# The up projection's gated convolution, four tiles at a time instead of two

## The chip, the cores and the metric

One core of a Trainium2 chip runs the whole kernel in one launch. The metric is the device time of that launch in microseconds (us). The core has a TensorE (matrix products), a VectorE, a ScalarE, a GpSimd and a SyncE (here it only issues transfers); each takes its own queue of instructions in order and waits on semaphores for the others.

## The reference, cut to what matters

One layer of an encoder on 256 positions of width 2048, all in float32: a token mixer, then a convolutional gated MLP with 5504 hidden channels, then a last norm. The change is in the MLP:

```python
def conv_ffn(x, g_norm, w_up, conv_k, conv_b, w_down):
    h = rms_norm(x, g_norm)
    up = h @ w_up                                   # 2048 -> 2 x 5504
    pad = jnp.pad(up, ((0, 0), (1, 1), (0, 0)))
    up = (pad[:, :t] * conv_k[0] + pad[:, 1:t + 1] * conv_k[1]
          + pad[:, 2:t + 2] * conv_k[2] + conv_b)   # width 3, over positions, each channel by itself
    gate, val = jnp.split(up, 2, axis=-1)
    return x + (jax.nn.silu(gate) * val) @ w_down
```

## The kernel before, in words

Every float32 operand of a product is split in two parts, a high part (rounded, `F32R`) and a low part (the rest), and three of the four products are summed. The activations' parts lie next to each other in SBUF. The weights are split as they come in, in pieces of 256 rows by 512 columns: SyncE loads a piece into `wraw` (five buffers), ScalarE copies the high part into `whi` (L171), VectorE subtracts it and writes the low part `wlo` (L172). There are four buffers each of `whi` and `wlo`; a piece is split three pieces ahead of its use.

The up stage works in 22 groups. A group takes the gate channels and the value channels of two neighbouring blocks of 128 (`nb` = 2; the last group has `nb` = 1), so four tiles of 128 channels by 256 positions, each in a PSUM bank of its own: columns 0 to 255 hold the sum for the high part of the activations (and, added to it, that of the low weights), columns 256 to 511 the sum for their low part. The contraction over 2048 goes in eight pieces; per piece there are high products (L223, 512 columns) and, every second piece, the low products of two pieces (L227, 256 columns). Eight banks let the next group start while the last is read out.

When a group's products are issued, `ev_up` reads its banks out and queues the rest as tasks of later pieces. For two blocks b = 0, 1, each with its gate tile and its value tile:

- read out, at once: ScalarE copies the second half of a bank into `tb`, VectorE adds the first half into `ta` (L1064, L1066), four times.
- `conv(0)` one piece into the next group, `conv(1)` three pieces into it (five in the last group): VectorE multiplies a tile by the norm's factor of each position (`rs["rb"]`, L1072), ScalarE makes the middle tap with the bias into `tc` (L1074), VectorE adds the two outer taps (L1077, L1079), for the two tiles of the block.
- `gate(b)` one piece after it: ScalarE applies SiLU (L1084), VectorE multiplies by the value tile (L1085).
- one piece later `split_plain` (L542, L543): the high and low part of the result, as activations of the down projection.
- for 13 of the pairs of blocks (`DOWN_PAIRS`) the sums that the down projection's faster scheme of multiplying 2 x 2 blocks needs are made two pieces after the gate (`act_blocks`, L324 to L327), split a piece later into the tile `so` and written to memory on GpSimd's queue (L1099).

Between these lie jobs that split some of the down projection's weights ahead of time (`split_ahead`): in eight groups a load on GpSimd's queue, then four additions on VectorE (L1296) at the pieces 6 and 7 of that group and 0 and 1 of the next, and two splits (L1301, L1302) at its pieces 2 and 4, by way of the same tile `so`.

The order of every engine's queue is the order in which the code issues. At each piece `begin` first issues the loads, then the split of the piece three ahead, then the tasks of this piece, and then the piece's products follow:

Of the kernel before, what the change touches and what calls it, by code (L numbers as in the profile page):

```python
# [8 lines left out]
F32 = mybir.dt.float32  # L9
BF16 = mybir.dt.bfloat16  # L10
F32R = mybir.dt.float32r
AF = mybir.ActivationFunctionType
OP = mybir.AluOpType
# [3 lines left out]
T = 256  # L17
# [8 lines left out]
NF = DFF // 128  # L26
# [53 lines left out]
def trunk_kernel(ctx, tc, x, x_t, vecs, w_in, ln_g, ln_b, w_st, b_s, rpb, w_branch, w_out, w_up, w_down,  # L80
                 norm_final, out):
    nc = tc.nc
    ctx.enter_context(tc.manual_schedule())

    def pool(name, side="left", bufs=1, space=None):
        kw = {} if space is None else {"space": space}
        st = ExitStack()
        p = st.enter_context(tc.tile_pool(name=name, bufs=bufs, side=side, reuse_waits="tile", **kw))
        return p, st
# [11 lines left out]
    turns, turns_st = pool("turns")  # L101
    turns = {"p": turns}
# [87 lines left out]
    def at(i, f):  # L190
        tasks.setdefault(i, []).append(f)

    cur = [0]
# [128 lines left out]
    def act_blocks(w, a11, a21, a12, a22):  # L322
        s3, n1, p2, s4 = (w[:, n * 128:(n + 1) * 128] for n in range(4))
        nc.vector.tensor_sub(s3, a11, a21)  # L324
        nc.vector.tensor_sub(n1, a22, a21)
        nc.vector.tensor_add(p2, n1, a11)
        nc.vector.tensor_sub(s4, a12, p2)  # L327
# [149 lines left out]
    ck = const.tile([128, 4, 2 * NF], F32)  # L477
# [63 lines left out]
    def split_plain(p, dst):  # L541
        nc.scalar.activation(dst[:, 0, :], p, AF.Copy)  # L542
        nc.vector.tensor_sub(dst[:, 1, :], p, dst[:, 0, :].bitcast(F32))  # L543
# [26 lines left out]
    def first_room(name, dt):  # L570
        return ypool.tile([128, 2, 512], dt, name=f"y{first_rooms.index('t13' if name == 'f' else name)}")
# [409 lines left out]
    rs = {}  # L981
# [73 lines left out]
    ff = {}  # L1055

    def ev_up(f0, nb):
        def done(ps, i):
            n = nb
            a = []  # L1060
            own = {}
            for p in ps:
                t = turns["p"].tile([128, T], F32, name="tb", bufs=3)
                nc.scalar.activation(t, p[:, T:], AF.Copy)  # L1064
                u = turns["p"].tile([128, T], F32, name="ta", bufs=6)
                nc.vector.tensor_add(u, p[:, :T], t)  # L1066
                a.append(u)

            def conv(b):
                c = []  # L1070
                for u, ch in ((a[b], f0 + b), (a[n + b], NF + f0 + b)):
                    nc.vector.tensor_mul(u, u, rs["rb"])  # L1072
                    v = ff["p"].tile([128, T], F32, name="tc", bufs=4)
                    nc.scalar.activation(v, u, AF.Identity, scale=ck[:, 1, ch:ch + 1], bias=ck[:, 3, ch:ch + 1])  # L1074
                    c.append((u, v, ch))
                for u, v, ch in c:
                    nc.vector.scalar_tensor_tensor(v[:, 1:], u[:, :T - 1], ck[:, 0, ch:ch + 1], v[:, 1:],  # L1077
                                                   op0=OP.mult, op1=OP.add)
                    nc.vector.scalar_tensor_tensor(v[:, :T - 1], u[:, 1:], ck[:, 2, ch:ch + 1], v[:, :T - 1],  # L1079
                                                   op0=OP.mult, op1=OP.add)  # L1080
                at(cur[0] + 1, lambda: gate(b, c[0][1], c[1][1]))

            def gate(b, g, v):
                nc.scalar.activation(g, g, AF.Silu)  # L1084
                nc.vector.tensor_mul(g, g, v)  # L1085
                at(cur[0] + 1, lambda: split_plain(g, ff["a"][f0 + b]))
                own[b] = g
                if b and f0 // 2 in ff["kept"]:
                    at(cur[0] + 2, sums)
                    at(cur[0] + 3, sums_split)  # L1090

            def sums():
                own["w"] = ff["more"].tile([128, 512], F32, name="sw")
                act_blocks(own["w"], *(own[k][:, t * 128:(t + 1) * 128] for k in range(2) for t in range(2)))

            def sums_split():
                o = ff["more"].tile([128, 2, 512], F32R, name="so")
                split_plain(own["w"], o)
                nc.gpsimd.dma_start(ff["kept"][f0 // 2], o.bitcast(F32))  # L1099

            at(i + 1, lambda: conv(0))
            if n > 1:
                at(i + (5 if f0 + 3 == NF else 3), lambda: conv(1))
        return done


# [107 lines left out]
    def sums_room(name, dt):  # L1214
        return s_room["p"].tile([128, 2, 512], dt, name=name)
# [15 lines left out]
    for n, (q, i, j) in enumerate(X_SUMS):  # L1231
        sum_acts_at(i, j, first_sums[2 * q], lambda q=q: q,
                    lambda name, dt, i=i: first_room("s2" if name == "f" and i < 16 else name, dt), f"s{n}", True)
# [17 lines left out]
    def split_read(kept, g, tile_of, queue=nc.gpsimd):  # L1251
        def read(pair, box, n):
            u = box.setdefault("u", [])
            u.append([tile_of(pair, p + n) for p in "hl"])
            for t, src in zip(u[-1], kept[pair, g][n]):
                queue.dma_start(t.bitcast(F32), src)
            if len(u) == 2:
                split_sums(box, u)
        return read

    def kept_sums(pair, box):
        held = [s for p, s in gate_held.values() if p == pair]
        if held:
# [11 lines left out]
                 split=(GATE_SPLIT[br], split_read(g_kept, br, lambda pair, name: sums_room("k" + name, F32R), nc.sync)))  # L1275
# [55 lines left out]
    for n, (pair, g) in enumerate((pair, g) for g in range(2) for pair in OUT_SPLIT[g]):  # L1331
        t_kept[pair, g] = split_rows("out", pair, g)
        i = g_at[2 * n][1]
# [46 lines left out]
    for n, q in enumerate(OUT_PAIRS):  # L1380
        i = g_m2[0][1] + OUT_SUMS[n]
# [3 lines left out]
    for f in range(0, NF, 2):  # L1385
        nb = min(2, NF - f)
# [17 lines left out]
    def down_order(g):  # L1404
# [7 lines left out]
                 split=({p: (6, 6) for p in DOWN_SPLIT}, split_read(d_kept, g, down_split_tile))) for g in range(2)]  # L1412
    ff["kept"] = {p: dram.tile([128, 2, 512], F32, name=f"sums{p}") for p in DOWN_PAIRS}
    for p, turn in zip(DOWN_SPLIT, DOWN_JOBS):
        for g in range(2):
            d_kept[p, g] = split_rows("down", p, g)
            i = g_up[turn[g]][1]
# [181 lines left out]
```

## Time and profile before

| what | us |
|---|---|
| device time, median of 3 runs | 1292.7 (1292.57 to 1293.34) |
| profiled execution, first to last instruction (span) | 1291.3 |
| TensorE busy | 1281.6 (99%) |
| VectorE busy | 1143.6 (89%) |
| ScalarE busy | 815.7 (63%) |
| GpSimd busy | 174.5 (14%) |
| up stage after its first group, 609 to 1066 us: TensorE, VectorE, ScalarE busy | 457.0, 407.5, 281.2 |

The profile is one execution, taken by the hardware profiler; of that execution only the span is known, and 1.4 us lie between it and the median of the timed runs. Times in its rows are us from the first instruction. PE is TensorE's products, PEld its weight loads, DVE VectorE, ACT ScalarE, POOL GpSimd, SP SyncE. A row of the timeline gives start, duration, engine, line, instruction, output<-inputs, shapes and count; in brackets the idle time before it and who ended it. Neighbouring instructions of an engine overlap a little, so a row of two is shorter than twice a row of one. A row of the groups gives the count, then busy us and the mean ns of one, then the idle time before them by who ended it. A row of the waits gives who waited for whom, us in all, times, and the longest.

### The profile page before, as it was taken

How to read it: one execution, taken by the hardware profiler on the slowest of the kernel's cores; microseconds unless marked ns; L12 is line 12 of the kernel's file. 1: busy time of each engine (PE TensorE's matmuls, PEld its weight loads, DVE VectorE, ACT ScalarE, POOL GpSimd, SP SyncE). 2: the span in 40 equal slices, each digit the busy share in tenths (PEclk: the TensorE clock that was granted, in tenths of full speed). 3: DMA queues.
4: the chain of work that ended last, by engine and by line, in shares of the span. 5: the costliest groups of instructions: out<-in, count | busy, mean ns of one | idle time of the engine just before them, and what ended most of it. 6: DMA issues, size and time to landing. Idle time of an engine off the chain costs nothing.

```text
span 1291.3 us, 19690 instructions
## 1 busy us (share of the span) xinstructions
PE 1281.6 (99%) x6653; PEld 1092.7 (85%) x6653; DVE 1143.6 (89%) x1712; ACT 815.7 (63%) x1229; POOL 174.5 (14%) x309
## 2 busy tenths in 40 slices
PE   9999999999999999999999999999999999999997
PEld 7888888888888888888888888888888888888885
DVE  7898978888889988996888899998988989989987
ACT  7776577877855655566566656566665656555554
POOL 0003706334000001100001001100000001211210
PEclk9999999999999999999999999999999999999999
DMA  9779879998799977965588788888877859998993
GB/s 368 273 272 282 289 236 306 322 316 300 275 335 349 353 244 244 412 225 164 182 295 274 239 297 290 270 267 285 266 220 222 279 171 363 368 388 325 353 383 146
DMA packets 199893, 369.51 MB, mean 286 GB/s; under 512 B 15984, under 2 KB 124144, under 8 KB 199792
## 3 DMA queue, kind: packets, MB, share of 16 engines
q1 hardware_dynamic: 175472, 286.36, 64.6%
q0 software_dynamic: 23888, 81.23, 17.8%
q8 instruction: 52, 0.85, 0.3%
q10 hardware_dynamic: 432, 0.66, 0.1%
q14 instruction: 49, 0.40, 0.1%
HBM read 320.48 MB, written 45.61 MB: 284 GB/s over the span
## 4 chain that ended last, share of the span: by engine, by line
PE 98%; DVE 1%; issue 0%; DVEq 0%; ACT 0%; ACTq 0%
PE bank L223 31%; PE bank L227 16%; PE bank L320 12%; PE bank L318 12%; PE bank L319 12%; PE bank L251 5%; PE bank L253 5%; PE bank L252 5%; PE bank L835 1%; DVE wlo L172 0%; PE bank L885 0%; PE bank L499 0%; PE bank L699 0%; PE bank L875 0%; PE bank L973 0%
## 5 line engine op out<-in xcount | busy, mean ns | idle before, releaser
L172 DVE TENSOR_TENSOR wlo<-wraw,whi 128x1024 fp32r<-128x1024 f32 (+1 forms) x472 | 537.0, 1151 | 98.2 <-ACT whi L171 64.2
L171 ACT ACTIVATE whi<-wraw 128x1024 fp32r<-128x1024 f32 (+1 forms) x472 | 463.3, 995 | 187.9 <-PE bank L319 72.4
L223 PE MATMUL bank<-h,whi 128*128 128x512 f32 x1760 | 425.5, 392 | 0.0
L223 PEld LDWEIGHTS bank<-h,whi 128*128 128x128 f32 x1760 | 322.0, 188 | 61.8
L227 PEld LDWEIGHTS bank<-h,wlo 128*128 128x128 f32 x1760 | 225.9, 191 | 8.8
L227 PE MATMUL bank<-h,wlo 128*128 128x256 f32 x1760 | 228.6, 283 | 0.0
L1074 ACT ACTIVATE tc<-ta,ck 128x256 f32<-128x256 f32 x86 | 47.1, 595 | 110.0 <-DVE ta L1072 110.0
L320 PE MATMUL bank<-wlo,a 128*128 128x512 f32 x188 | 73.4, 390 | 0.2 <-DVE wlo L172 0.2
L318 PE MATMUL bank<-whi,h 128*128 128x512 f32 x186 | 73.2, 394 | 0.0
L318 PE MATMUL bank<-whi,a 128*128 128x512 f32 x188 | 73.2, 389 | 0.0
L319 PE MATMUL bank<-whi,a 128*128 128x512 f32 x188 | 73.1, 389 | 0.0
L319 PE MATMUL bank<-whi,h 128*128 128x512 f32 x186 | 72.8, 391 | 0.0
L320 PE MATMUL bank<-wlo,h 128*128 128x512 f32 x186 | 72.6, 390 | 0.0
L1077 DVE SCALAR_TENSOR_TENSOR tc<-ta,ck,tc 128x255 f32<-128x255 f32 x86 | 41.4, 481 | 14.4 <-ACT tc L1074 14.4
L800 POOL TENSOR_SCALAR_AFFINE_SELECT bias<-run 64x128 f32<-64x128 f32 x64 | 39.7, 654 | 85.4 <-DVE sc L843 84.7
L1306 POOL DMA_DIRECT2D down_h<-so x16 | 8.7, 545 | 311.1 <-ACT tc L1084 170.3
L251 PE MATMUL bank<-whi,y 128*128 128x512 f32 x128 | 50.6, 395 | 0.0
L251 PE MATMUL bank<-whi,h 128*128 128x512 f32 x128 | 50.4, 394 | 0.0
L253 PE MATMUL bank<-wlo,h 128*128 128x512 f32 x128 | 49.9, 390 | 0.0
L253 PE MATMUL bank<-wlo,y 128*128 128x512 f32 x128 | 49.9, 390 | 0.0
L252 PE MATMUL bank<-whi,y 128*128 128x512 f32 x128 | 49.8, 389 | 0.0
L252 PE MATMUL bank<-whi,h 128*128 128x512 f32 x128 | 49.8, 389 | 0.0
(332 smaller groups left out, 2075.7 us busy)
## 6 DMA issues: line engine op xcount, KB each, us to landing
wraw<-in_w_up_dram SPq DMA_DIRECT2D x336, 256.0 KB, 4.0
wraw<-in_w_in_dram SPq DMA_DIRECT2D x107, 512.0 KB, 6.3
wraw<-in_w_down_dram SPq DMA_DIRECT2D x78, 512.0 KB, 7.3
wraw<-in_w_in_dram SPq DMA_DIRECT2D x70, 256.0 KB, 6.0
wraw<-in_w_branch_dram SPq DMA_DIRECT2D x32, 512.0 KB, 5.7
wraw<-in_w_out_dram SPq DMA_DIRECT2D x28, 512.0 KB, 6.1
h<-sums POOLq DMA_DIRECT2D x18, 512.0 KB, 7.6
tw<-in_w_down_dram POOLq DMA_DIRECT2D x8, 1024.0 KB, 8.3
```

The lines of the kernel that those rows point to most:

```text
L171: nc.scalar.activation(h[:, k, :m], w[:, k, :m], AF.Copy)
L172: nc.vector.tensor_sub(l[:, k, :m], w[:, k, :m], h[:, k, :m].bitcast(F32))
L223: nc.tensor.matmul(p, h[:, k - k0, b * 128:(b + 1) * 128], acts(k), start=k == 0, stop=k == nk - 1)
L227: nc.tensor.matmul(p[:, :T], l[:, k - k0, b * 128:(b + 1) * 128], acts(k)[:, 0, :], start=False, stop=False)
L251: nc.tensor.matmul(p, xh, h[:, kk, :m], start=st, stop=False)
L252: nc.tensor.matmul(p, xl, h[:, kk, :m], start=False, stop=False)
L253: nc.tensor.matmul(p, xh, l[:, kk, :m], start=False, stop=sp)
L318: nc.tensor.matmul(p, xh, h, start=st, stop=False, **kw)
L319: nc.tensor.matmul(p, xl, h, start=False, stop=False, **kw)
L320: nc.tensor.matmul(p, xh, l, start=False, stop=sp, **kw)
L1074: nc.scalar.activation(v, u, AF.Identity, scale=ck[:, 1, ch:ch + 1], bias=ck[:, 3, ch:ch + 1])
L1077: nc.vector.scalar_tensor_tensor(v[:, 1:], u[:, :T - 1], ck[:, 0, ch:ch + 1], v[:, 1:], op0=OP.mult, op1=OP.add)
```

## The change

The four tiles of a group go through the tail together. The copies from the banks go straight into one tile `ta` of 128 x 4 x 256 (one buffer instead of six, and no `tb`), and the additions are in place. One piece into the next group the four tiles are multiplied by the norm's factors in one operation, with the row of factors repeated by a step of zero, and ScalarE makes the four middle taps into one tile `tc` (one buffer). At the second piece VectorE adds the first outer tap of all four tiles, then the second of all four, and ScalarE's SiLU on both gate tiles at once follows in the same task. At the third piece come one product of gates and values and one copy of the high parts, at the fourth one subtraction for the low parts; for the kept pairs the sums at the fifth and their splitting and writing at the sixth, each a piece earlier than before. The last full group is no exception any more.

```diff
     def ev_up(f0, nb):
         def done(ps, i):
...
-            for p in ps:
-                t = turns["p"].tile([128, T], F32, name="tb", bufs=3)
-                nc.scalar.activation(t, p[:, T:], AF.Copy)
-                u = turns["p"].tile([128, T], F32, name="ta", bufs=6)
-                nc.vector.tensor_add(u, p[:, :T], t)
-                a.append(u)
...
-            at(i + 1, lambda: conv(0))
-            if n > 1:
-                at(i + (5 if f0 + 3 == NF else 3), lambda: conv(1))
+            u = turns["p"].tile([128, 2 * nb, T], F32, name="ta", bufs=1)
+            for n, p in enumerate(ps):
+                nc.scalar.activation(u[:, n], p[:, T:], AF.Copy)
+                nc.vector.tensor_add(u[:, n], p[:, :T], u[:, n])
+            box = {}
+            channels = [f + b for f in (f0, NF + f0) for b in range(nb)]
+
+            def scale():
+                rb = rs["rb"]
+                nc.vector.tensor_mul(u, u, bass.AP(tensor=rb.tensor, offset=rb.offset,
+                                                   ap=[rb.ap[0], [0, 2 * nb], [1, T]]))
+                v = box["v"] = ff["p"].tile([128, 2 * nb, T], F32, name="tc", bufs=1)
+                for n, ch in enumerate(channels):
+                    nc.scalar.activation(v[:, n], u[:, n], AF.Identity, scale=ck[:, 1, ch:ch + 1],
+                                         bias=ck[:, 3, ch:ch + 1])
+
+            def conv():
+                v = box["v"]
+                for tap, to, of in ((0, slice(1, T), slice(0, T - 1)), (2, slice(0, T - 1), slice(1, T))):
+                    for n, ch in enumerate(channels):
+                        nc.vector.scalar_tensor_tensor(v[:, n, to], u[:, n, of], ck[:, tap, ch:ch + 1], v[:, n, to],
+                                                       op0=OP.mult, op1=OP.add)
+                nc.scalar.activation(v[:, :nb], v[:, :nb], AF.Silu)
+
+            def gate():
+                v = box["v"]
+                nc.vector.tensor_mul(v[:, :nb], v[:, :nb], v[:, nb:])
+                a = ff["ap"][f0 // 2]
+                nc.scalar.activation(a[:, :, 0, :], v[:, :nb], AF.Copy)
+
+            def split():
+                v, a = box["v"], ff["ap"][f0 // 2]
+                nc.vector.tensor_sub(a[:, :, 1, :], v[:, :nb], a[:, :, 0, :].bitcast(F32))
...
+            steps = [scale, conv, gate, split]
+            if f0 // 2 in ff["kept"]:
+                steps += [sums, sums_split]
+            for n, step in enumerate(steps):
+                at(i + 1 + n, step)
         return done
```

`sums` and `sums_split` do what they did, on the new tile.

More of the change, by code (lines that the diff above doesn't have):

```diff
@@ L1058, in done @@
         def done(ps, i):
-            n = nb
-            a = []
-            own = {}
-            for p in ps:
-                t = turns["p"].tile([128, T], F32, name="tb", bufs=3)
-                nc.scalar.activation(t, p[:, T:], AF.Copy)
-                u = turns["p"].tile([128, T], F32, name="ta", bufs=6)
-                nc.vector.tensor_add(u, p[:, :T], t)
-                a.append(u)
[L1069 to L1090, printed above, removed]
+            u = turns["p"].tile([128, 2 * nb, T], F32, name="ta", bufs=1)
+            for n, p in enumerate(ps):
+                nc.scalar.activation(u[:, n], p[:, T:], AF.Copy)
+                nc.vector.tensor_add(u[:, n], p[:, :T], u[:, n])
@@ L1092, in sums @@
+            def split():
+                v, a = box["v"], ff["ap"][f0 // 2]
+                nc.vector.tensor_sub(a[:, :, 1, :], v[:, :nb], a[:, :, 0, :].bitcast(F32))
             def sums():
-                own["w"] = ff["more"].tile([128, 512], F32, name="sw")
-                act_blocks(own["w"], *(own[k][:, t * 128:(t + 1) * 128] for k in range(2) for t in range(2)))
+                v = box["v"]
+                box["w"] = ff["more"].tile([128, 512], F32, name="sw")
+                act_blocks(box["w"], *(v[:, k, t * 128:(t + 1) * 128] for k in range(2) for t in range(2)))
@@ L1096, in sums_split @@
             def sums_split():
                 o = ff["more"].tile([128, 2, 512], F32R, name="so")
-                split_plain(own["w"], o)
+                split_plain(box["w"], o)
                 nc.gpsimd.dma_start(ff["kept"][f0 // 2], o.bitcast(F32))
-            at(i + 1, lambda: conv(0))
-            if n > 1:
-                at(i + (5 if f0 + 3 == NF else 3), lambda: conv(1))
+            steps = [scale, conv, gate, split]
+            if f0 // 2 in ff["kept"]:
+                steps += [sums, sums_split]
```

## The prediction, made before the change was run

> **What bounds the kernel now.** I read the page first, then who waited for whom, the stage by itself, one group in order of time, and last the margins.
>
> ```profile
> span 1291.3 us, 19690 instructions
> PE 98%; DVE 1%; issue 0%; DVEq 0%; ACT 0%; ACTq 0%
> PE bank L499 <- DVE one L489: 1.5, 1, 1.5
> PE bank L320 <- DVE wlo L172: 0.2, 1, 0.2
> 609.00:1066.00 457.00, 457.00 (x2630) 403.89 (x2629) 407.50 (x693) 281.19 (x446) 29.64 (x53) 1.00 0.78 254
> ```
>
> The first two lines are the page's span and its chain of work: TensorE carries 98% of it. The next two are all the waits of TensorE in the run, 1.7 us. The last is the up stage after its first group (busy us of PE, weight load, DVE, ACT, POOL): TensorE is busy in all 457.0 us, VectorE in 407.5, ScalarE in 281.2. So no saving on VectorE or ScalarE can shorten this stage. The change can only do nothing or make TensorE wait, and the question is how much delay the split weights bear. They come three pieces ahead, and both engines take their queues in order. Here is group 7 (counted from 0; its pieces P0 to P7).
>
> ```profile
> 743.78 1.22 DVE L172 TENSOR_TENSOR wlo<-wraw,whi 128x1024 fp32r<-128x1024 f32 x1
> 745.52 1.41 DVE L1066 TENSOR_TENSOR ta<-bank,tb 128x256 f32<-128x256 f32 x4
> 746.31 2.00 ACT L171 ACTIVATE whi<-wraw 128x1024 fp32r<-128x1024 f32 x2
> 746.84 2.08 PE L227 MATMUL bank<-h,wlo 128*128 128x256 f32 x16
> 747.39 2.36 DVE L172 TENSOR_TENSOR wlo<-wraw,whi 128x1024 fp32r<-128x1024 f32 x2 [0.47 <-ACT whi L171]
> 749.67 0.75 DVE L1072 TENSOR_TENSOR ta<-ta,rb 128x256 f32<-128x256 f32 x2
> 750.12 1.10 ACT L1074 ACTIVATE tc<-ta,ck 128x256 f32<-128x256 f32 x2 [1.82 <-DVE ta L1072]
> 750.75 0.48 DVE L1077 SCALAR_TENSOR_TENSOR tc<-ta,ck,tc 128x255 f32<-128x255 f32 x1 [0.33 <-ACT tc L1074]
> 751.12 1.04 ACT L171 ACTIVATE whi<-wraw 128x1024 fp32r<-128x1024 f32 x1
> 751.27 0.48 DVE L1079 SCALAR_TENSOR_TENSOR tc<-ta,ck,tc 128x255 f32<-128x255 f32 x1
> 751.68 0.48 DVE L1077 SCALAR_TENSOR_TENSOR tc<-ta,ck,tc 128x255 f32<-128x255 f32 x1
> 752.07 0.40 ACT L1084 ACTIVATE tc<-tc 128x256 f32<-128x256 f32 x1
> 752.19 0.48 DVE L1079 SCALAR_TENSOR_TENSOR tc<-ta,ck,tc 128x255 f32<-128x255 f32 x1
> 752.38 1.05 ACT L171 ACTIVATE whi<-wraw 128x1024 fp32r<-128x1024 f32 x1
> 752.59 1.22 DVE L172 TENSOR_TENSOR wlo<-wraw,whi 128x1024 fp32r<-128x1024 f32 x1
> 753.73 0.42 DVE L1085 TENSOR_TENSOR tc<-tc 128x256 f32<-128x256 f32 x1
> 754.06 1.22 DVE L172 TENSOR_TENSOR wlo<-wraw,whi 128x1024 fp32r<-128x1024 f32 x1
> 756.96 1.05 ACT L171 ACTIVATE whi<-wraw 128x1024 fp32r<-128x1024 f32 x1
> 759.88 2.91 PE L223 MATMUL bank<-h,whi 128*128 128x512 f32 x12
> 762.63 2.08 PE L227 MATMUL bank<-h,wlo 128*128 128x256 f32 x16
> ```
>
> Three things to see. First, the two engines overlap: while VectorE runs the four taps (750.75 to 752.67), ScalarE copies the high half of P5 (751.12), so VectorE waits only 0.33 us per half group. Second, the margin: P7's high half is ready at 758.01; P7's first product is the ninth of the twelve from 759.88, 0.228 us apart, so 761.71: 3.7 us spare. (The group's first product is sixteen before 746.84, so at 743.2.) Third, what an instruction costs its queue is the distance to the next: 1.14 us for a 1024-wide split on VectorE (two in 2.36, one 1.22), 0.33 for a 256-wide add (four in 1.41) or product, 0.40 for a tap behind a tap on another tile (751.27 to 751.68), 0.52 behind one on its own tile (750.75 to 751.27); on ScalarE 0.95 for a high copy, 0.50 for the middle-tap copy (two in 1.10). A hand-over between the engines takes 0.03 to 0.04: the first of the two high copies from 746.31 ends at 747.36 (1.05), and its subtraction starts at 747.39.
>
> **The change part by part.**
>
> ```profile
> L223 PE MATMUL bank<-h,whi 128*128 128x512 f32 x1314 | 314.2, 391 | 0.0
> L227 PE MATMUL bank<-h,wlo 128*128 128x256 f32 x1312 | 170.5, 283 | 0.0
> ```
>
> A product alone takes 0.391 us, twelve take 2.91, so they come 0.228 apart; a low one takes 0.283, sixteen 2.08, so 0.120. A group has 64 of each: 22.26 us. Twenty groups and the half-size last one, in whose time the tails run, need 20 x 22.26 + 11.13 = 456.3 us.
>
> Queues after the change, P3's split on. VectorE: P3, P4, scale, P5, eight taps, P6, gate product, P7, low half. ScalarE: P3, P4, four middle-tap copies, P5, SiLU, P6, high copy, P7. Every step of the chain now waits for the other engine, and a weight split stands behind each.
>
> ```profile
> L172 DVE TENSOR_TENSOR wlo<-wraw,whi 128x1024 fp32r<-128x1024 f32 x158 | 192.3, 1221 | 29.1 <-ACT whi L171 12.2 <-PE bank L227 8.8 <-issue 7.8
> L1296 DVE TENSOR_TENSOR tw<-tw 128x512 f32<-128x512 f32 x32 | 21.9, 684 | 0.0
> L1302 DVE TENSOR_TENSOR tw<-tw,so 128x1024 fp32r<-128x1024 f32 x16 | 19.5, 1219 | 0.0
> L543 DVE TENSOR_TENSOR so<-sw,so 128x512 fp32r<-128x512 f32 x13 | 8.9, 683 | 0.0
> L542 ACT ACTIVATE so<-sw 128x512 fp32r<-128x512 f32 x13 | 8.2, 632 | 14.8 <-DVE sw L327 14.8
> 742.72 0.28 DVE L324 TENSOR_TENSOR sw<-tc 128x128 f32<-128x128 f32 x1
> down_h<-so POOLq DMA_DIRECT2D x16, 512.0 KB, 3.7
> ```
>
> VectorE's work per group. Unchanged: eight splits 8 x 1.14 = 9.12, four adds 1.33. Scale: four at 0.33 become one 1024 wide, taken at a split's 1.14 (the repeated row of factors is new; it could cost 0.2 more, or nothing, and I take the row of the same size and kind). Taps: 4 x (0.52 + 0.40) = 3.68 become 8 x 0.40 = 3.2, since no tap follows one on its own tile. Gate product and low half: two each of 0.33 become one each of 0.60 (0.684, less the 0.08 by which neighbours overlap). Before 16.8, after 16.0 us: 0.8 us less work. A kept pair's sums add 1.06 (742.72 to 743.78) + 0.60 in 13 of the 21 tails, a splitting job for the down projection 4 x 0.60 + 2 x 1.14 = 4.7 in each of 8; both unchanged.
>
> VectorE's waits per group. Before: twice 0.33. After, from where VectorE could issue on:
> (a) scale to P5: 0.08 (its end) + 0.04 + four middle-tap copies 2.02 + P5's copy 1.05 + 0.04 = 3.2. Nothing else stands between on VectorE, the taps come after P5.
> (b) taps to P6: SiLU needs the gate halves, done with the sixth tap. From its start 0.48 + 0.04 + SiLU 0.53 (as the 512-wide copy's 0.632, less 0.10 of overlap) + 1.05 + 0.04 = 2.14, less three taps' 1.20: 0.9.
> (c) gate product to P7: 0.08 + 0.04 + high copy 0.53 + 1.05 + 0.04 = 1.7.
> Together 5.9 instead of 0.7.
>
> The ledger: before, 21 x 17.5 + 13 x 1.66 + 8 x 4.7 = 426.7, less 4.3 for the last group's half-size splits (8 x 0.54): 422 of 456.3, so 34 us to spare; the trace's row has 29.1 us of idle before the splits, so the ledger holds. After: 21 x 21.9 + 59.2 - 4.3 - 1.3 (its shorter copies) = 513.5. That is 57 us more than TensorE needs, and TensorE pays it, as every split is behind the chain.
>
> A light group (no sums, no job), walked from its first product: P0's low products end 4.8 us on and free the buffer for P4's subtraction; 4.84 + 1.14 (P4) + 1.14 (scale) + 3.2 = 10.35 for P5; + 1.14 + 3.2 + 0.9 = 15.6 for P6, whose copy ended at 15.57 against a need at 16.7; + 1.14 + 0.68 + 0.04 + 0.53 = 18.0 for P7's copy, which ends at 19.0 against 18.5. So even there 0.55 us is lost, though the ledger (21.9) shows 0.36 spare. In a group with a job's splits two adds (1.2) stand ahead of the scale and a subtraction (1.14) ahead of the taps, and VectorE comes 0.9 later to P4: P6 is 1.5 late and P7 another 1.7. Walked like this group by group: 0.6 and 0.8 us in groups 1 and 3; 3.2 in 2, 4, 6, 10, 14 and 18; 4.8 in 8 and 12, behind a kept pair and a job's first adds; 2.7 in 5, 7, 9, 11, 13, 15 and 19; 1.25 in 16, 17 and 20; 5.6 in the last, with half the time for the same tail. Together 58 us: the lead of three pieces is a credit once, the waits for TensorE's buffers take a little more. Forecast: the profiled span 1291.3 + 58 = 1349; the median of the runs lies 1.4 above this span, 1292.7 + 58 = 1351 us.
>
> Edits taken at nothing. ScalarE's copy lands in the tile that VectorE adds in place: parts of one tile don't wait for each other here,
>
> ```profile
> 17.58 0.89 ACT L558 ACTIVATE h<-xr 128x256 fp32r<-128x256 f32 x2
> 18.85 0.87 DVE L561 SCALAR_TENSOR_TENSOR h<-xr,h 128x256 fp32r<-128x256 f32 x2
> ```
>
> where ScalarE fills both high parts of a tile before VectorE begins the first low part. One buffer each for ta and tc: the next group writes them after the taps and sums are long done; the cover is six pieces. The sums and their DMA on POOL's queue come one piece earlier, two pieces (5.6 us) behind a job's write out of the same tile so, which lands in 3.7 us; if that cover went, the seven groups with both would lose up to 1.5 us each, +10. SP's loads only move later with the splits. The last pair no longer has its second half put off to P5; in the 11 us group behind it the same three waits cost 5.6, in the sum.
>
> By the Trainium skill (Perfetto Trace Analysis, Optimizing Scalar/DVE Operations) grouping into larger operations helps when the engine is saturated, and where an unsaturated engine makes bubbles elsewhere, breaking instructions up can let work finish sooner; this stage, with VectorE at 407.5 of 457.0, is the second case: by the second rule the sum has the sign of mine, by the first alone it would be 0.
>
> Bounds. Hand-overs of 0.02 to 0.06 instead of 0.04, six of them a group: -3 to +3. The 512-wide ScalarE operations at 0.40 instead of 0.53: -0.26 a group, -5. P5's copies overlapping more than I allow, 0.3 a group: -6. Together down to +44 (1336). Up: the so tile +10, and rival 1.
>
> **Rivals.**
> 1. SiLU waits for all eight taps (the wait may be set for the last write to the tile). Then (b) is 0.08 + 0.04 + 0.53 + 1.05 + 0.04 = 1.7, +0.8 x 21 = +17: 1368 us. For it: SiLU reads two tiles' worth in one piece. Against: the rows of line 558.
> 2. Not slower: the new waits fall into VectorE's spare time, 34 us plus 0.8 x 21 saved. TensorE stays full, 1292.7 us. It decides at a total of new waits of 51 us, 2.4 a group, and I count 5.2; wait (a) would have to be gone, if P5's copy came before the middle-tap copies. Against: both engines' rows above stand in the order in which the code issues. By the grouping rule above this rival holds.
> 3. The clock.
>
> ```profile
> 1.47 4.02 PE L499 MATMUL bank<-h 128*128 128x512 bf16 x9 [1.47 <-DVE one L489]
> 4.93 0.99 PE L318 MATMUL bank<-whi,h 128*128 128x512 f32 x1
> ```
>
> At the start, after idling, products come 0.38 us apart (nine from 1.47 to 4.93), later 0.228. My pauses are 1 to 2.7 us, at P6 and at P7. If each made the 3.7 us of products behind it 1.68 times slower, 2.5 us a group, half hidden in the next pause: +25, 1376 us. The Trainium skill (TensorE: Matmul & The Clock Gate, Part 1) has the clock halved after an idle window of about 3.4 us; by that rule my pauses are too short and the sum stays.
> 4. Part of it: cheaper chains than any row shows, +3 to +43.
>
> **How the numbers follow.** Forecast (1336 to 1361) 0.70; rival 1 0.14; rival 2 0.05; rival 3 0.06; rival 4 0.05. Time 1351. Range 1336 to 1371: it takes in rival 1 and leaves out 2, 4 and most of 3, under 2 in 10. About 0.2% is what a measurement tells from no change: slower 0.94, same 0.04, faster 0.02 (a gain would need a gap in TensorE to close, and there is none).
>
> **What the changed profile would show.** TensorE waiting for ScalarE's whi at P6 and P7 of nearly every group, 55 us or so in all, by the chain of waits two in a group; the middle-tap copies waiting for the scale and VectorE's wlo waiting for whi, 5 to 6 us a group (some 120 us in all); a group every 22.8 us where light and about 25 where sums or a job's splits fall; the stage at about 535 us instead of 477; the stages before and after unchanged. TensorE without waits, or SiLU starting after the eighth tap's end, would show me wrong in the sum or in (b); products more than 0.23 us apart after a pause, rival 3.

## The result, and the profile after

The changed kernel takes 1356.6 us (median of 4 runs, 1355.4 to 1357.3) against 1292.7: 1.049 times as long (95% interval 1.048 to 1.0505). Its profiled execution has a span of 1354.6 us, 63.3 more than before. The forecast was +58: the direction and the mechanism came as it had them, and 5.3 us of the span are to be explained. Of the experiments below, one of the eleven timed executions of e1 took 3323 us, for a reason that was not found; it stands in no ratio.

The page of the changed kernel: its span, the busy time of each engine and the chain of work that ended last.

```profile
span 1354.6 us, 19526 instructions
PE 1297.9 (96%) x6653; PEld 1095.2 (81%) x6653; DVE 1127.1 (83%) x1606; ACT 806.3 (60%) x1187; POOL 175.5 (13%) x309
PE 78%; DVE 8%; ACT 6%; issue 4%; DMA 3%; ACTq 0%; DVEq 0%; SPq 0%; POOL 0%; POOLq 0%
```

VectorE is busy 16.5 us less than before and ScalarE 9.4 less: the change does save the work that it takes out. But the chain of work, 98% TensorE before, now leaves TensorE for more than a fifth of the span.

Who waited for whom, before (the whole run),

```profile
DVE wlo L172 <- ACT whi L171: 64.2, 93, 2.0
```

and after:

```profile
DVE wlo L172 <- ACT whi L171: 179.1, 149, 3.1
ACT tc L1072 <- DVE ta L1068: 85.8, 22, 5.4
ACT tc L1081 <- DVE tc L1079: 78.2, 21, 4.0
PE bank L223 <- ACT whi L171: 46.3, 37, 2.4
ACT a L1087 <- DVE tc L1085: 42.9, 22, 3.6
ACT so L542 <- DMA down_h<-so: 21.4, 7, 3.2
```

ScalarE waits for VectorE at each of the three followers (L1072, L1081, L1087), VectorE waits for the high copies queued behind them, and TensorE waits 46.3 us for those copies, 37 times, where it waited for none. In one group, group 7, in order of time:

```profile
766.50 1.22 DVE L1068 TENSOR_TENSOR ta<-ta,rb 128x1024 f32<-128x1024 f32 x1
767.76 2.08 ACT L1072 ACTIVATE tc<-ta,ck 128x256 f32<-128x256 f32 x4 [3.04 <-DVE ta L1068]
769.74 1.04 ACT L171 ACTIVATE whi<-wraw 128x1024 fp32r<-128x1024 f32 x1
770.82 1.23 DVE L172 TENSOR_TENSOR wlo<-wraw,whi 128x1024 fp32r<-128x1024 f32 x1 [3.10 <-ACT whi L171]
771.96 3.24 DVE L1079 SCALAR_TENSOR_TENSOR tc<-ta,ck,tc 128x255 f32<-128x255 f32 x8
774.51 0.63 ACT L1081 ACTIVATE tc<-tc 128x512 f32<-128x512 f32 x1 [3.72 <-DVE tc L1079]
775.05 1.04 ACT L171 ACTIVATE whi<-wraw 128x1024 fp32r<-128x1024 f32 x1
776.12 1.23 DVE L172 TENSOR_TENSOR wlo<-wraw,whi 128x1024 fp32r<-128x1024 f32 x1 [0.91 <-ACT whi L171]
776.14 2.11 PE L223 MATMUL bank<-h,whi 128*128 128x512 f32 x8 [1.12 <-ACT whi L171]
777.26 0.69 DVE L1085 TENSOR_TENSOR tc<-tc 128x512 f32<-128x512 f32 x1
777.99 0.63 ACT L1087 ACTIVATE a<-tc 128x512 fp32r<-128x512 f32 x1 [1.90 <-DVE tc L1085]
778.52 2.94 ACT L171 ACTIVATE whi<-wraw 128x1024 fp32r<-128x1024 f32 x3
779.59 1.23 DVE L172 TENSOR_TENSOR wlo<-wraw,whi 128x1024 fp32r<-128x1024 f32 x1 [1.64 <-ACT whi L171]
779.61 1.20 PE L223 MATMUL bank<-h,whi 128*128 128x512 f32 x4 [1.36 <-ACT whi L171]
```

Read it as a zigzag. The scale ends at 767.72, ScalarE's four copies and the copy of P5 follow, and VectorE stands 3.10 us. Then the taps, SiLU, the copy of P6: 0.91. Then the gate product, the high copy, the copy of P7: 1.64. But for SiLU, which runs under the last two taps, the two engines are never at work on this tail at once. TensorE runs out of weights at P6 (776.14) and at P7 (779.61).

How long a group is, from its first high product to the next group's, is read from such boundaries; a full group's need is 22.26. The columns are the stretch and its length, then the busy us of PE, weight load, DVE, ACT and POOL, and last the granted clock, the DMA share and GB/s. Groups 3 and 8 of the changed kernel:

```profile
658.91:681.88 22.97, 22.54 (x129) 19.59 (x128) 17.32 (x25) 12.51 (x20) 0.71 (x1) 1.00 0.80 280
783.48:812.57 29.09, 25.79 (x130) 21.70 (x129) 23.37 (x36) 14.54 (x21) 2.70 (x5) 0.88 0.70 225
```

The first, a light group, is 0.7 us too long. The second, behind a kept pair and a job's first additions, is 6.8 too long, and its clock was 0.88. In the same way for all groups, with the forecast's walk beside it, and the last of the experiments below (the sums are of the unrounded lengths; the kernel before has 0.3 by the same reading):

| groups | forecast, each | changed kernel | e8 (own tile and early table) |
|---|---|---|---|
| 1 | 0.6 | 2.1 | 0.8 |
| 3 | 0.8 | 0.7 | 0.7 |
| 2, 4, 6, 10, 14, 18 | 3.2 | 3.1 each | 3.1 each |
| 8, 12 | 4.8 | 6.8, 4.9 | 4.8 each |
| 5, 7, 11, 13, 15, 19 | 2.7 | 2.8 to 3.3, 18.3 in all | 2.4 each |
| 9 | 2.7 | 1.2 | 2.4 |
| 16, 17, 20 | 1.25 | 1.2 each | 1.2 each |
| last | 5.6 | 7.0 | 6.9 |
| sum | 58.4 | 63.4 | 56.8 |

### The profile page after: what moved, and what is told of

Same layout as the page of the kernel before. It is cut to its first block, busy times and chain, and to the rows that moved or that the text cites. A ratio compares the mean times of both kernels' runs of the same rounds, so it can differ in the third digit from the quotient of the medians.

```text
span 1354.6 us, 19526 instructions
## 1 busy us (share of the span) xinstructions
PE 1297.9 (96%) x6653; PEld 1095.2 (81%) x6653; DVE 1127.1 (83%) x1606; ACT 806.3 (60%) x1187; POOL 175.5 (13%) x309
## 4 chain that ended last, share of the span: by engine, by line
PE 78%; DVE 8%; ACT 6%; issue 4%; DMA 3%; ACTq 0%; DVEq 0%; SPq 0%; POOL 0%; POOLq 0%
PE bank L223 20%; PE bank L320 11%; PE bank L319 11%; PE bank L318 11%; PE bank L227 10%; PE bank L251 4%; PE bank L253 4%; PE bank L252 4%; ACT whi L171 4%; DVE wlo L172 3%; ACT tc L1072 2%; DVE tc L1079 2%; DMA wraw<-in_w_up_dram 1%; DVE ta L1068 1%; DMA down_h<-so 1%
## 5 line engine op out<-in xcount | busy, mean ns | idle before, releaser
L223 PE MATMUL bank<-h,whi 128*128 128x512 f32 x1760 | 437.9, 397 | 46.5 <-ACT whi L171 46.3
L1072 ACT ACTIVATE tc<-ta,ck 128x256 f32<-128x256 f32 x86 | 44.8, 590 | 85.8 <-DVE ta L1068 85.8
L318 PE MATMUL bank<-whi,h 128*128 128x512 f32 x186 | 73.0, 392 | 0.0
L319 PE MATMUL bank<-whi,h 128*128 128x512 f32 x186 | 72.4, 389 | 0.0
L1079 DVE SCALAR_TENSOR_TENSOR tc<-ta,ck,tc 128x255 f32<-128x255 f32 x172 | 69.8, 479 | 0.0
L1081 ACT ACTIVATE tc<-tc 128x512 f32<-128x512 f32 (+1 forms) x22 | 13.7, 622 | 78.3 <-DVE tc L1079 78.2
L251 PE MATMUL bank<-whi,h 128*128 128x512 f32 x128 | 50.4, 394 | 0.0
```

The lines of the kernel that those rows point to most:

```text
L223: nc.tensor.matmul(p, h[:, k - k0, b * 128:(b + 1) * 128], acts(k), start=k == 0, stop=k == nk - 1)
L251: nc.tensor.matmul(p, xh, h[:, kk, :m], start=st, stop=False)
L318: nc.tensor.matmul(p, xh, h, start=st, stop=False, **kw)
L319: nc.tensor.matmul(p, xl, h, start=False, stop=False, **kw)
L1072: nc.scalar.activation(v[:, n], u[:, n], AF.Identity, scale=ck[:, 1, ch:ch + 1], bias=ck[:, 3, ch:ch + 1])
L1079: nc.vector.scalar_tensor_tensor(v[:, n, to], u[:, n, of], ck[:, tap, ch:ch + 1], v[:, n, to], op0=OP.mult, op1=OP.add)
```

## The experiments

Three theories were set against each other. **A, the order:** the time is lost because ScalarE's follower of every VectorE step is issued in the same task, ahead of a weight's high copy; issued a piece later it would find its input ready. **B, the width:** it is lost because each operation is 512 or 1024 wide, so that nothing can follow before all four tiles are done. **C, the buffers:** it is lost because `ta` and `tc` have one buffer each.

### e1: all three followers one piece later, operations as wide as in the change

```diff
             def scale():
                 ...
-                v = box["v"] = ff["p"].tile([128, 2 * nb, T], F32, name="tc", bufs=1)
-                for n, ch in enumerate(channels):
-                    nc.scalar.activation(v[:, n], u[:, n], AF.Identity, scale=ck[:, 1, ch:ch + 1],
-                                         bias=ck[:, 3, ch:ch + 1])
             def conv():
+                v = box["v"] = ff["p"].tile([128, 2 * nb, T], F32, name="tc", bufs=1)
+                for n, ch in enumerate(channels):
+                    nc.scalar.activation(v[:, n], u[:, n], AF.Identity, scale=ck[:, 1, ch:ch + 1],
+                                         bias=ck[:, 3, ch:ch + 1])
-                v = box["v"]
                 ...
-                nc.scalar.activation(v[:, :nb], v[:, :nb], AF.Silu)
             def gate():
+                nc.scalar.activation(v[:, :nb], v[:, :nb], AF.Silu)
                 nc.vector.tensor_mul(v[:, :nb], v[:, :nb], v[:, nb:])
-                a = ff["ap"][f0 // 2]
-                nc.scalar.activation(a[:, :, 0, :], v[:, :nb], AF.Copy)
             def split():
                 ...
+                nc.scalar.activation(a[:, :, 0, :], v[:, :nb], AF.Copy)
```

> The wide operations of the changed kernel stay as they are; only ScalarE's three followers (middle taps, SiLU, high copy) are issued one piece later than the VectorE operation that they wait for, so a weight copy goes ahead of each. Theory A (order: a weight copy queued behind a ScalarE operation that waits for VectorE): all three round trips leave the path of the splits, the ledger falls to about 16 us of work with 0.3 us of wait per group beside the sums and jobs, TensorE has no waits in the up stage: 1292.7, as before the change, within 1 us. Theory B (width: an operation over four tiles ends too late for whoever needs its first tile): the width is the same, so most of the 64 us stays, 1340 or more. Theory C (one buffer for ta and tc): the tiles are held one piece longer at most, so no better than the change, 1356.

Measured: 1293.8 us, 1.001 times before (1.0001 to 1.0019); span 1291.2. The groups of the stage, first of the changed kernel (609 to 1129 us) and then of e1 (609 to 1066 us):

```profile
L223 PE MATMUL bank<-h,whi 128*128 128x512 f32 x1313 | 326.4, 398 | 46.5 <-ACT whi L171 46.3
L172 DVE TENSOR_TENSOR wlo<-wraw,whi 128x1024 fp32r<-128x1024 f32 x159 | 192.6, 1222 | 119.2 <-ACT whi L171 116.8 <-DMA wraw<-in_w_up_dram 2.4
```

```profile
L223 PE MATMUL bank<-h,whi 128*128 128x512 f32 x1312 | 313.6, 391 | 0.0
L172 DVE TENSOR_TENSOR wlo<-wraw,whi 128x1024 fp32r<-128x1024 f32 x158 | 192.2, 1220 | 58.2 <-issue 32.9 <-ACT whi L171 14.6 <-PE bank L227 8.2
```

TensorE's idle time ahead of the high products falls from 46.5 us to 0.0, and VectorE's wait for the copies from 116.8 to 14.6, where the kernel before has 12.2. With the order mended at most 0.2% is left of the loss, at the same width and with the same buffers, so B and C fall as causes by themselves. What the width adds in the change's own order is left to e5. It also answers why the change wins nothing with its order mended: the work that it saves lies on engines that TensorE does not wait for.

### e2, e3, e4: one follower alone a piece later

Each has one of the three moves of e1: e2 the middle-tap copies (wait a), e3 SiLU (wait b), e4 the high copy (wait c).

> Only the four middle-tap copies are moved, from the scale's task to the start of the taps' task one piece later, behind P5's weight copy; SiLU and the high copy stay where the change has them. Theory A: wait (a), 3.2 us a group, goes, and with it nearly the whole loss, because the other two waits (2.6 us a group) fit into what VectorE has to spare: 1296, with pauses left in groups 8, 12 and 21 only (0.7, 1.6 and 0.9 us by the walk along the queues). Theory B: 1340 or more. Theory C: 1356.

> Only SiLU is moved, from the end of the taps' task to the start of the gate's, behind P6's weight copy. Theory A: P6's copy no longer waits for the taps, but the gate product now waits for SiLU; walked along the queues 41 us are left of 64: 1334. Theory B: 1356, the widths are the same. Theory C: 1356.

> Only the high copy is moved, from the gate's task to the start of the low half's, behind P7's weight copy. Theory A: P7's copy no longer waits for the gate product; walked along the queues 20 us are left of 64: 1313, with TensorE's pauses at P6 instead of P7. Theory B: 1356. Theory C: 1356.

| kernel | wait taken away | median us | ratio to before (95%) | gain over the changed kernel |
|---|---|---|---|---|
| e2 | (a) 3.10 | 1298.3 | 1.0043 (1.0029 to 1.0057) | 58 |
| e4 | (c) 1.64 | 1318.3 | 1.0198 (1.0183 to 1.0214) | 38 |
| e3 | (b) 0.91 | 1336.0 | 1.0337 (1.0323 to 1.0351) | 21 |

TensorE's waits for the high copy, in e2, in e3 and in e4:

```profile
PE bank L223 <- ACT whi L171: 3.5, 4, 1.3
```

```profile
PE bank L223 <- ACT whi L171: 28.3, 16, 3.2
```

```profile
PE bank L223 <- ACT whi L171: 16.6, 16, 2.4
```

The three gains add up to 117 us, though only 64 are to be had: the waits share one spare. The forecast's ledger had 2.4 us a group to spare, and TensorE pays what goes beyond it. The three waits are 5.65; without (a) 2.55 are left, about the spare, and nearly all is gone. The rule is rough: without (c) 4.0 are left and without (b) 4.7, by which e4 and e3 would lose 34 and 49 us over 21 groups; read by groups they lost 24 and 44. The times expected were 2 us too low for e2 and e3 and 5 for e4. In e2 the half-size last group lost 2.5 us where the expectation had 0.9; what e3 and e4 missed was not followed up.

### e5: the order of the change, every wide operation cut into one for each tile

```diff
-                nc.vector.tensor_mul(u, u, bass.AP(tensor=rb.tensor, offset=rb.offset,
-                                                   ap=[rb.ap[0], [0, 2 * nb], [1, T]]))
+                for n in range(2 * nb):
+                    nc.vector.tensor_mul(u[:, n], u[:, n], rb)
...
-                nc.scalar.activation(v[:, :nb], v[:, :nb], AF.Silu)
+                for n in range(nb):
+                    nc.scalar.activation(v[:, n], v[:, n], AF.Silu)
```

and likewise the gate product, the high copy and the low half.

> The changed kernel's order and tasks, with each wide operation cut back into operations on one tile (four scale products, two SiLU, two gate products, two high copies, two low halves). Theory A with hand-over by tiles: the order still puts the weight copies behind ScalarE's waits, but a follower starts after the first tile and not after all, so wait (a) falls from 3.2 to 2.2 us, (b) and (c) by 0.3 to 0.5; walked along the queues 38 us are left of 64: 1331. So of the loss about 26 us would be the width in this order, 38 the order alone. Theory B (width alone): 1293. Order alone with no part for the width: 1356.

Measured: 1332.9 us, 1.0306 (1.0289 to 1.0324); span 1332.8. The waits of e5 in the stage:

```profile
DVE wlo L172 <- ACT whi L171: 95.9, 75, 2.1
ACT tc L1072 <- DVE ta L1069: 69.0, 22, 4.7
PE bank L223 <- ACT whi L171: 27.7, 29, 2.0
```

The first copy can follow the first tile's scale, and VectorE's longest wait for a copy is 2.1 instead of 3.1 us. So of the 64 us some 40 are the order's with narrow operations, and width adds 24, in this order; in e1's order it adds nothing beyond 0.2%. The Trainium skill (Perfetto Trace Analysis, Optimizing Scalar/DVE Operations) has it that breaking instructions up may help where unsaturated engines make bubbles in others. The runs agree for this order, 1356.6 against 1332.9; e1 shows a cure that the section does not name, with the operations left whole.

### e6: two buffers for `tc`

```diff
-                v = box["v"] = ff["p"].tile([128, 2 * nb, T], F32, name="tc", bufs=1)
+                v = box["v"] = ff["p"].tile([128, 2 * nb, T], F32, name="tc", bufs=2)
```

> The changed kernel with two buffers for the tile tc instead of one (there is no room for two of ta as well). Theory A: no wait of the chain is for a buffer, 1356. Theory C (one buffer makes the next group's middle taps wait for the last reader of the tile before): 1340 or less, and the middle-tap copies would wait less than their 3 to 5 us.

Measured: 1356.0 us, 1.0488 (1.0467 to 1.0509), no different from the changed kernel (1.048 to 1.0505). A second buffer for `ta` was not tried; e1 keeps one of each and loses nothing.

### e7 and e8: the two small terms by themselves

Both keep the change's order and width. The job's splits get a high tile of their own, and one tiny SiLU is issued earlier, to bring SiLU's table in: in e7 at piece 4 of group 0 (the diff shows this), in e8 at its piece 7.

```diff
-            split_ahead(w_d, d_kept, lambda: ff["more"], lambda c: "so", nc.gpsimd, p, g, g * 1024, i, range(i + 6, i + 10), (i + 10, i + 12), 0)
+            split_ahead(w_d, d_kept, lambda: ff["more"], lambda c: "sj", nc.gpsimd, p, g, g * 1024, i, range(i + 6, i + 10), (i + 10, i + 12), 0)
...
+    at(g_up[0][1] + 4, lambda: nc.scalar.activation(one, one, AF.Silu))
```

> The changed kernel, with SiLU's table loaded by one tiny SiLU during the first group, and with a tile of their own for the jobs' high halves, so that the sums' split no longer waits for a job's write out of the tile so. Theory A with these two as the part that the prediction lacked: group 1's loss falls from 2.1 to 0.6 us, those of 5, 7, 11, 13, 15 and 19 from 2.9 to 3.3 to about 2.4, the rest stays: 1350 to 1352. If they were hidden: 1356.

> As the kernel before (SiLU's table loaded early by one tiny SiLU, a tile of their own for the jobs' high halves), but the tiny SiLU three pieces later, at the first group's last piece, behind the norm's square root, which had loaded its own table in between so that SiLU's came back into the chain. If the table load in the chain is what group 1 lost beyond the walk: its loss falls from 2.1 to 0.6 us, the other groups stay at 2.4 to 4.8, the last at 7.0; 1351. If not: group 1 stays at 2.1, 1352.5.

Measured: e7 1352.5 us, 1.0462 (1.0446 to 1.0477); e8 1350.0, 1.0447 (1.043 to 1.0465). The tile came out as expected in both, 2.4 us lost in groups 5, 7, 9, 11, 13, 15 and 19. The table did not in e7: group 1 stayed at 2.1. Its timeline says why:

```profile
599.58 1.28 ACT L1534 ACT_TABLE_LOAD   x1
602.05 1.28 ACT L506 ACT_TABLE_LOAD   x1
623.96 1.28 ACT L1081 ACT_TABLE_LOAD   x1 [3.71 <-DVE tc L1079]
```

The tiny SiLU's load at 599.58 was undone 2.5 us later by that of the norm's square root (L506), and SiLU loaded its table again in group 1. In e8 the tiny one comes behind the root, and SiLU in group 1 needs none:

```profile
606.60 1.28 ACT L1534 ACT_TABLE_LOAD   x1
623.51 0.63 ACT L1081 ACTIVATE tc<-tc 128x512 f32<-128x512 f32 x1 [3.72 <-DVE tc L1079]
```

Group 1 then loses 0.8, where the forecast had 0.6.

## Why the prediction was right, and where it was off

**What bounds, and the direction.** Right: no saving on VectorE or ScalarE showed up anywhere, not even in e1, where it is all that is left of the change.

**The three waits.** Forecast 3.2, 0.9 and 1.7, measured 3.10, 0.91 and 1.64 in group 7: 5.65 instead of the 5.9 in the sum. The taps came 0.40 apart, as assumed for taps that do not follow one on their own tile.

**The walk by group.** With the two small terms taken out, in e8, 56.8 us are lost against the walk's 58.4, and the walk is right within 0.35 us in every group but the last. The ledger's sum hides this: it was the walk that knew that a light group loses something and that groups 8 and 12 lose 4.8. One sign was misread: the stage, from its first high product to the next stage's first, takes 481.0 us before and 544.2 after, not 477 and 535; it is 63.2 longer, where these two are 58 apart.

**Rival 1.** Wrong, as held: the first tap of the group starts at 771.96, so the sixth, 0.40 apart and 0.48 long, ends at 774.44, and SiLU starts at 774.51. The eighth ends at 775.20.

**Rival 2.** Its point of decision held: waits of 2.4 us a group would be free, and (a) would have to be gone. e2 is that kernel: 2.55 left, 1298.3 us.

**Rival 4.** Wrong: no wait was shorter than forecast by more than 0.1 us, and the time is 64 us over the kernel before, outside its +3 to +43.

**TensorE's waits, 55 us or so.** 46.3 in the trace. The other part is in its busy time, which grew by 16.3: ahead of each of 37 pauses the last product counts with its full 0.391 instead of the 0.228 to the next one, 6.0 in all. Of the remaining 10 some 6 are products at half the clock (rival 3), and 4 the first product behind each pause, whose next comes 0.11 us later than usual: the eight from 776.14 take 2.11 us, where at 0.228 apart they would take 1.99.

**Steps that were mis-sized.** Four terms:

1. *The tile `so`, under "edits taken at nothing".* Its cover did not hold. It was to be two pieces, 5.6 us, for a write that lands in 3.7. Group 7 after the change:

```profile
755.51 0.53 POOL L1310 DMA_DIRECT2D down_h<-so  x1 [7.93 <-ACT so L1305]
759.16 0.29 DVE L327 TENSOR_TENSOR sw<-tc,sw 128x128 f32<-128x128 f32 x1
760.15 0.63 ACT L542 ACTIVATE so<-sw 128x512 fp32r<-128x512 f32 x1 [3.04 <-DMA down_h<-so]
```

   The sums are done at 759.45, only 3.9 us after the write was issued, because VectorE, late, runs through its queue without gaps; the write lets the tile go 4.6 us after its issue, and ScalarE copies 0.7 us later than it could. Both sizes were off: the median from issue to landing of these writes is 4.5 us in the changed kernel, and 3.7 would still have fitted. Groups 5, 7, 11, 13, 15 and 19 lose 18.3 us here and 14.3 in e7, 0.67 each; with group 9 at the same price that is 4.7 us. The bound given was 10. In e1 this same wait for the write is still there (20.5 us in all) and costs nothing, as nothing of TensorE's hangs on it.
2. *SiLU's table, not in the sum at all.* Before, its load of 1.28 us stood in group 1 too, from 618.11, and the group lost 0.1 us in all. After the change it stands in the chain between the taps and P6's copy:

```profile
623.28 1.28 ACT L1081 ACT_TABLE_LOAD   x1 [3.71 <-DVE tc L1079]
626.18 1.23 DVE L172 TENSOR_TENSOR wlo<-wraw,whi 128x1024 fp32r<-128x1024 f32 x1 [2.19 <-ACT whi L171]
```

   Wait (b) is 2.19 there instead of 0.91, and e8 against e7 puts its price in group 1 at 1.3 us. Before, nothing on TensorE's path waited for the load, so its row was in no ledger.
3. *The last group:* 7.0 instead of 5.6. Its last products come at half the clock (below), which by their distances costs 1.4 us; without it the walk's 5.6 is left.
4. *Seven groups behind a kept pair,* 2.4 instead of 2.7 once `so` is out: the walk was 2.2 us too dear in all.

Items 1 to 3 are +4.7, +1.3 and +1.4, item 4 -2.2, and the six groups at 3.1 instead of 3.2 another -0.5: +4.7 on 58.4, so 63.1 of the 63.4 measured; that terms of both signs offset each other is luck. The time between span and median was 2.0 us, not 1.4.

**Rival 3, the clock.** Its mechanism is there and its price, +25, was not. Group 8 of the changed kernel, and the same pause in e7:

```profile
803.18 2.75 PE L223 MATMUL bank<-h,whi 128*128 128x512 f32 x8 [2.42 <-ACT whi L171]
```

```profile
802.26 2.11 PE L223 MATMUL bank<-h,whi 128*128 128x512 f32 x8 [2.42 <-ACT whi L171]
```

After the pause of 2.42 us the changed kernel's products slow down within these eight, to 0.43 us apart, until 811; in e7 they do not. Group 8 loses 6.8 instead of 4.8. But the engines behind catch up meanwhile: group 9 loses 1.2 instead of 2.4, and the pair 8.0 instead of the 7.1 of e7, of which `so` is 0.7. The clock was halved three times in the changed kernel, not behind each pause: in group 12 it left 4.9 instead of e8's 4.8, and only in the last group, which no other group follows, does it stay. Eight of its low products before the clock is halved at 1125.28, and its last eight:

```profile
1119.82 1.11 PE L227 MATMUL bank<-h,wlo 128*128 128x256 f32 x8
1126.65 1.91 PE L227 MATMUL bank<-h,wlo 128*128 128x256 f32 x8
```

## What to carry to other kernels

Before making operations wider, ask whether an engine that waits needs the time saved; here 98% of the chain of work was TensorE's, and VectorE's 16.5 us went nowhere. On queues taken in order, put the follower on the other engine a step behind its producer, not right after it: a follower issued early holds up whatever stands behind it, and the price is, roughly, what the waits exceed the spare by, not their sum. When a new chain becomes the bound, look again at everything that used to be hidden on it: a shared tile's write, an activation table.

## What the runs showed of the hardware that was not expected

- Pauses of TensorE of 2.4 us were at times followed by some microseconds at half the clock, with products 0.43 us apart instead of 0.228. Which pauses are followed by it can be read from the granted clock. In the changed kernel's up stage it is halved at 804.43, 906.83 and 1125.28 us, which are 30 and 64 times 3.413 us apart, for 6.83, 3.41 and 3.41 us: it changes at the ends of windows of 3.413 us that follow each other through the whole stage. Below are the window ahead of 804.43 and the slow stretch, and then of e7 the two windows on which the same pause falls, counted back from 903.71 us, where its own clock is first halved (busy us of PE first, the granted clock third from the end):

```profile
801.02:804.43 3.41, 1.25 (x5) 1.05 (x6) 2.50 (x6) 1.57 (x2) 0.00 (x0) 1.00 0.82 321
804.43:811.26 6.83, 6.11 (x21) 4.89 (x20) 5.16 (x8) 4.42 (x5) 1.07 (x2) 0.50 0.54 174
```

```profile
797.89:801.31 3.42, 1.95 (x17) 1.75 (x15) 3.42 (x9) 0.68 (x2) 0.53 (x1) 1.00 0.84 275
801.31:804.72 3.41, 2.11 (x8) 1.42 (x8) 1.84 (x3) 1.51 (x3) 0.00 (x0) 1.00 0.51 193
```

  The pause of 2.42 us leaves TensorE idle for 2.16 us of one window in the changed kernel; in e7 a window's end divides it, and the windows have 1.47 and 1.30 us of idle time. So it goes in the up stages of all ten runs: behind each of the 13 windows at full clock with 1.87 us or more of idle time the clock was halved, behind none with 1.72 or less, and behind four of the five between. Where in the windows a pause falls is chance. The Trainium skill (TensorE: Matmul & The Clock Gate, Part 1) has the clock halved after an idle window of about 3.4 us, and the window free-running; the traces agree with such a window, but one that is a little over half idle was enough. Taken as a pause of that length, as the prediction took it, the runs disagree with it.
- A square root between two SiLUs costs SiLU a second load of its table, 1.28 us (e7). The Trainium skill (ScalarE activation tables: per-element evaluation and per-set limits, What a function is on this engine) puts two functions of different sets one load of 1283 ns apart; the trace agrees.
